# Starting the operands of the 512-column products at multiples of 512 bytes in each SBUF partition

## The chip, the cores and the metric

The kernel runs on one core of a Trainium2 chip. The metric is the time of one execution on the device in microseconds (us); lower is better. SBUF is the on-chip memory: 128 partitions, each a row of bytes, in which every tile of this program has a start address that is the same in all partitions. TensorE (PE in the profile) reads both operands of a product from there.

## The reference

One decoder layer over 2,048 tokens of width 1,024 and 16 meta tokens put ahead of them, all in float32:

```python
h = layer_norm(jnp.concatenate([meta, x], axis=1), ln_in_g, ln_in_b)
mix = hybrid_mixer(h, ...)      # sliding-window attention || gated linear attention, then w_out
h = layer_norm(ALPHA * h + mix, ln1_g, ln1_b)
ffn = swiglu(h, w_gate, w_up, w_down)       # silu(h @ w_gate) * (h @ w_up) @ w_down, width 2816
h = layer_norm(ALPHA * h + ffn, ln2_g, ln2_b)
return h[:, N_META:]
```

The mixer projects every token to 2,320 columns (queries, keys and values of both kinds of attention, an output gate and a low-rank decay gate), runs window attention with eight query heads over a window of 128 tokens and gated linear attention with four heads in chunks, and projects the 1,024 joined columns with w_out.

## The kernel before, in words

**Products in three parts.** Each float32 operand is split into a high part (fp32r) and the rest (`split_into`, L177 to L179: ScalarE writes the high part, VectorE or GpSimd the difference). A product is then three matmuls per 128 rows of the contraction: high by high, high by low, low by high (`matmuls`, L183 to L186, is the one place that issues them, so nearly all carry the line L186 in the profile). A matmul names the stationary operand, 128 columns or 512 bytes of a partition, which a weight load (PEld) brings into the array, and then the moving operand, in most cases 512 columns or 2,048 bytes, that streams through it.

**Stages.** Window attention comes first (to about 430 us): for each block of 512 tokens the products `pu` of the projections, whose moving operand is `h` and whose stationary one is `hl_u`. Linear attention with the output projection follows (to about 1,000 us; `pv`, `po` with 256 or 272 columns, and `pu` again, now on `gh`). The gate and up products of the feed-forward layer run from there to 1,861 us, for two halves of the tokens and 11 pairs of column tiles each; they use seven quarter products (Strassen's method in Winograd's form) with the factors b11, t2, t1, b21, t3, t4, b22 of the tokens as moving operands, in this order, and the weights' factors `pa..`, `ps..` as stationary ones. One quarter product is two chains of 12 matmuls. The last stage is the down projection (1,874 to 2,359 us), with the products `d`: moving operand `B` (weights), stationary operand `A` (activations), and for the pair left over `E`, which holds both.

**Where tiles lie.** The program takes its tiles from pools, and these are stacked in SBUF: most from the left, that is from the end of a scratch area for DMA descriptors at address 0 upwards, some from the right (`side="right"`), from byte 229,344 downwards. A tile takes a multiple of 32 bytes. On the left come, in this order:

- the scratch area, 16,384 bytes, and four constants of the framework with 32 bytes each;
- `cp`: `ident` 512, `neghalf`, `half` and `warm` 32 each, `hm` 1,024, `kTm` 128, in all 1,760 bytes;
- `wpool` (L190) with the staging tiles `x` and the split weights `whl` (tiles `hl_..`, `pa..`, `ps..`, `B`), and `hb` (L209) with two tiles of 16,384 bytes, in turn the tokens `h` and `gh` and the factors b11 and t2. All of these are multiples of 512 bytes, so they begin at 16,384 + 128 + 1,760 = 18,272 = 35 x 512 + 352 and keep the remainder 352;
- after them the pools of the stage: `gp` (4,416 bytes with constants), then `hp1` (L254) with the tokens of every second block; later `fp` and `hop1` (factors t1, b21), and in the last stage `rp` (21,120 bytes) and `dp` with `rA`, `A` and `E`.

On the right lie `gm` (the mixed heads `msh`, `msl`) and, in the gate and up stage, `hop2` (t3, t4) and `hop3` (b22). 229,344 is 447 x 512 + 480.

So each operand of the 512-column products has a remainder on division by 512 (all of them leave 32 on division by 64):

| operand | pool | remainder before |
|---|---|---|
| stationary weights `hl_u`, `pa`, `ps`; moving `B` | wpool | 352 |
| moving `h` of blocks 0 and 2, `gh`, b11, t2 | hb | 352 |
| moving `h` of blocks 1 and 3 | hp1 | 160 |
| moving t1, b21 | hop1 | 352 |
| moving t3, t4, b22 | hop2, hop3 | 480 |
| stationary `A`; both operands in `E` | dp | 480 |

**In the names of the profile**, `t<-h_t,ps` are the products of t2, t1 (remainder 352) and t3 (480), `b<-h_b,pa` those of b11 and b21 (352), `t<-h_t,pa` those of t4 (480) and `b<-h_b,ps` those of b22 (480).

**The order of the work.** The steps of the attention stages are strings written by hand (L36 to L47), and the order on each engine comes from a planner that simulates the program (`schedule_with_timeline_sim=True`). With `reuse_waits="tile"` a tile of a new pool waits for the tiles of an older pool whose bytes it covers.

Of the kernel before, what the change touches and what calls it, by code (L numbers as in the profile page):

```python
# [14 lines left out]
P = 128  # L15
# [12 lines left out]
LEVELS = [64, 32, 16, 8, 4, 2]  # L28
UNITS = ["k_s", "v_s", "q_s0", "q_s1", "q_s2", "q_s3", "q_g0", "q_g1", "k_g0", "k_g1", "r0", "r1", "r2", "r3"]

# The order of the steps for one block of tokens, each with its number.
# Window attention: q projection of a head pair (q this block's, Q the next one's), K keys (0) and
# values (1) of the next block, S scores and V values of a group of heads, L load of a token tile,
# G projection for the linear attention.
WINDOW_STEPS = "G0 L0 S0 V0 q3 S1 L1 L2 q2 S2 V1 G3 S3 G2 G1 V2 L3 K0 V3 Q0 Q1 K1"
# Linear attention: k a chunk's next part; of the next block H load, a and b values, g gate, c its sums,  # L36
# r output gate, m meta tokens; of this block S and G the mixed heads; of the block before
# x output projection, y norm, z transposition; C factors and F first steps of the feed-forward layer.
# [6 lines left out]
# The first products of the feed-forward layer, and what is left of the last block after each.  # L45
# [36 lines left out]
def host_layout(inp):  # L82
# [15 lines left out]
    # the low rank part of the gate, then the values  # L98
# [12 lines left out]
    # quarters (f half, k half) of each pair of f tiles, gate and up side by side  # L111
    gu = np.stack([f(n)[0].reshape(2, KT // 2, P, NP, 2, P) for n in ("w_ffn_gate", "w_ffn_up")])
    a["w_gu"] = gu.transpose(4, 5, 1, 3, 0, 2, 6).reshape(NP, 2, 2, P, D)
    # quarters (f half, output half) of each pair of f tiles
# [7 lines left out]
def body(ctx, tc, t, seq):  # L122
# [34 lines left out]
    def moments(sm, xt, n, name):  # L157
        """-mean * rstd, rstd"""
        st = sm(f"st_{name}", [P, 2, 6])
        for c in range(2):  # L160
            nc.vector.bn_stats(st[:n, c, :], xt[:n, c * 512 : (c + 1) * 512])
        mv = sm(f"mv_{name}", [P, 2])
        nc.vector.bn_aggr(mv[:n], st[:n].rearrange("p a b -> p (a b)"))
        v = sm(f"lv_{name}", [P, 1])
        nc.vector.tensor_scalar(v[:n], mv[:n, 1:2], EPS_LN, None, op0=ALU.add)
        r = sm(f"lr_{name}", [P, 1])
        nc.gpsimd.tensor_tensor(r[:n], v[:n], neghalf[:n, 0:1], op=ALU.pow)
        m = sm(f"lm_{name}", [P, 1])
        nc.vector.tensor_scalar(m[:n], mv[:n, 0:1], r[:n, 0:1], -1.0, op0=ALU.mult, op1=ALU.mult)
        return m, r  # L170

    def normalise(sm, xt, n, name, mr=None):
        """(x - mean) * rstd in place"""
        m, r = mr or moments(sm, xt, n, name)
        nc.scalar.activation(xt[:n], xt[:n], AF.Identity, bias=m[:n, 0:1], scale=r[:n, 0:1])

    def split_into(hi, lo, src, lo_eng=None):  # L177
        nc.scalar.activation(hi, src, AF.Copy)  # L178
        (lo_eng or nc.vector).tensor_tensor(lo, src, r32(hi), op=ALU.subtract)  # L179

# [8 lines left out]
    kTm = cp.tile([P, 2, NM], F32, name="kTm")  # L189
    wpool = ctx.enter_context(tc.tile_pool(name="wpool", bufs=1))  # L190
# [17 lines left out]
    # two halves of 16 KB a partition: a block's tokens by k's halves, then factors, then results  # L208
# [5 lines left out]
    def at(h, a, k):  # L214
        """part a of the tokens' rows k.."""
        return h[k // 4][:, a, k % 4]
# [35 lines left out]
    # ------------------------------------------- input norm and sliding window  # L252
    with ExitStack() as c1:
        hps = [hb, c1.enter_context(tc.tile_pool(name="hp1", bufs=1))]  # L254
        mp = c1.enter_context(tc.tile_pool(name="mp", bufs=1))
# [46 lines left out]
        # a head's values have zeros beside them, in the place of the other head's  # L302
        vhl = [mp.tile([P, NB, 3, 64], F32R, name=f"v{x}") for x in "hl"]
        # the keys of a block and the block before share their slots: what a slot holds
        # of the block before is weighed with the difference of the two blocks' values
# [80 lines left out]
        def begin(u, h):  # L386
            """the first half of a projection, before the other half's tokens are there"""
# [28 lines left out]
        def k_write(raw, n, w, c0, c1_):  # L416
            """both halves of the keys' parts, from [128 (head, d), n * w]"""
# [65 lines left out]
        def swa_scores(s, k, qs):  # L483
            """four heads of two token tiles; a head pair's keys and values lie side by side"""
# [114 lines left out]
    # --------------------------------------------- gated linear attention, output projection  # L599
    # The feed-forward products are taken by quarters, in the seven  # L600
    # multiplications of Strassen's method in Winograd's form.  The tokens'
    # factors: b11, b21, b22 are quarters (k half, token half), t2 = b22 - b12 + b11,
    # t1 = b12 - b11, t3 = b22 - b12, t4 = b21 - t2.
# [7 lines left out]
    def quarter(tb, kh, th, k, n):  # L611
        """rows k.. of one quarter of the tokens, transposed"""
# [4 lines left out]
    def combine(tb, k, tile_):  # L617
        """the sums and differences among the factors, for one of the rows"""
# [20 lines left out]
    def make(f, tb):  # L639
        """a factor of the tokens' side, in its two parts"""  # L640
# [72 lines left out]
    class Mixed:  # L713
        """the mixed heads, in two parts each, and their projection, step by step"""
# [75 lines left out]
    class Project:  # L790
        """the projections of the linear attention for one block of tokens, step by step"""
# [42 lines left out]
        def values(self, blk, n):  # L834
            """the values of one token tile, or of the meta tokens"""
# [39 lines left out]
        def m(self, _):  # L875
            """the state after the meta tokens"""
# [144 lines left out]
    def start_ffn(n):  # L1021
        """the first factors of the feed-forward layer, and the first product"""
# [11 lines left out]
    def take(what, *who):  # L1034
        """one step, of the first that has it; nothing where there is no such block"""
        for x in who:
            if hasattr(x, what[0]):
                return getattr(x, what[0])(int(what[1]))
# [30 lines left out]
    # ------------------------------------------------------------- ffn, gate and up  # L1069
    banks = [0]  # L1070

    def bank(name):
        """the next of the eight banks in turn"""
# [5 lines left out]
    # products of the down projection, in the order taken  # L1079
# [18 lines left out]
    def a_factors(tb, p0, npr):  # L1098
        """the factors of the activations, by tokens' and f's halves"""
# [4 lines left out]
    def combined(b11, b12, b22, b21, t1):  # L1104
        """the factors of the weights, by f's and outputs' halves, one after the other"""
# [20 lines left out]
    def odd_factors(tb):  # L1126
        """the factors of the pair left over, of the activations and of the weights side by side"""
# [15 lines left out]
    def residual(tb, n, i, j, tag):  # L1143
        """alpha times the first norm's output less its bias, one half of a token tile"""
# [7 lines left out]
    def finish(tb, n, i, y, sums, eng):  # L1152
        """norm of one token tile, g2 having the root of D in it"""
# [82 lines left out]
    # quarters of the result that a product ends  # L1236
# [17 lines left out]
    def start_down():  # L1254
        """what the down projection needs before its first product"""
        for n in ("rp", "dp"):
            pools[n] = hops2.enter_context(tc.tile_pool(name=n, bufs=1, reuse_waits="tile"))
        for x, src in (("g1", "ln1_g"), ("b1", "ln1_b"), ("g2", "ln2_g"), ("b2", "ln2_b")):
            rows_[x] = pools["rp"].tile([P, D], F32, name=x)
        for k in range(LOOK):  # L1260
# [42 lines left out]
    # the last block's steps after the first products  # L1303
# [8 lines left out]
    def finish_mixing(f):  # L1312
# [8 lines left out]
        ops.update({f: make(f, 0) for f in ("t3", "t4", "b22")})  # L1321

# [65 lines left out]
    # ------------------------------------------------------------------ ffn, down  # L1388
    pools["acc"] = hops2.enter_context(tc.tile_pool(name="accp", bufs=1, side="right", reuse_waits="tile"))
    ready_to = LOOK  # L1390
    for k, (tb, gi, q) in enumerate(STEPS):
        # of the activations' factors four fit, those left over counted
# [31 lines left out]
```

## Time and profile before

| what | value |
|---|---|
| median of 3 runs | 2394.92 us (2389.49 to 2397.25) |
| span of the profiled execution, first to last instruction | 2381.3 us |
| difference of the two, which lies around the span | 13.6 us |
| PE busy | 2212.6 us, 93%, 11,536 matmuls |
| VectorE busy | 1782.8 us, 75% |
| GpSimd busy | 1613.5 us, 68% |
| ScalarE busy | 957.8 us, 40% |
| mean granted TensorE clock | 0.972 |

The profiled execution has no device time of its own beside its span, so the median stands in for it. Matmuls overlap: the next one starts before the last one's results are out, and the end in the profile contains the way through the array. The pace of a run of matmuls is therefore read from starts: from the start of one group to the start of the next, divided by the number of matmuls between.

### The profile page before, as it was taken

The numbers are of one execution on the slowest core, as the hardware profiler recorded it, in microseconds if no ns is written. First come the engines' busy times: TensorE is split into PE (matmuls) and PEld (weight loads), VectorE is DVE, ScalarE is ACT, GpSimd is POOL, SyncE is SP. The second block draws the span as 40 slices with busy tenths as digits, with TensorE's granted clock in tenths as the row PEclk, the third lists the DMA queues.
The fourth block names the chain that finished last, engine by engine and source line by source line (L and its number), as shares of the span: only waits on it lengthen the run. The fifth ranks groups of instructions, "written<-read, shape, count | busy, mean of one in ns | idle before, by whom it ended". The sixth has DMA issues, their size and how long they took to land.

```text
span 2381.3 us, 32174 instructions
## 1 busy us (share of the span) xinstructions
PE 2212.6 (93%) x11536; PEld 1875.2 (79%) x11536; DVE 1782.8 (75%) x2653; ACT 957.8 (40%) x1606; POOL 1613.5 (68%) x1128
## 2 busy tenths in 40 slices
PE   6999999999999988998999999999999799878995
PEld 5888888888989877976888887888888688656774
DVE  6787765678778696467666667666666689999998
ACT  5565655544353535332222334222323433244332
POOL 6889865848366564565767777767667645895567
PEclk9999999999999999998999999999999899999998
DMA  8754631624363556455323344323223755445532
GB/s 272 231 173 143 213 128 50 214 76 169 126 242 112 213 175 246 167 186 183 124 75 125 106 139 140 129 75 124 97 103 106 267 157 162 135 147 178 175 98 84
DMA packets 169889, 361.01 MB, mean 152 GB/s; under 512 B 15697, under 2 KB 61682, under 8 KB 169730
## 3 DMA queue, kind: packets, MB, share of 16 engines
q1 hardware_dynamic: 165922, 356.51, 44.2%
q10 hardware_dynamic: 3808, 2.45, 0.3%
q8 instruction: 92, 1.51, 0.3%
q14 instruction: 67, 0.55, 0.1%
HBM read 247.22 MB, written 111.67 MB: 151 GB/s over the span
## 4 chain that ended last, share of the span: by engine, by line
PE 58%; DVE 22%; POOL 6%; issue 6%; DMA 5%; ACT 2%; SPq 0%; DVEq 0%; POOLq 0%; ACTq 0%
PE t L186 16%; PE b L186 11%; PE pu L186 8%; PE d L186 6%; PE po L186 6%; PE pv L186 3%; DVE y L1141 3%; DVE xq L963 2%; DVE B L179 2%; DVE A L179 1%; PE oa L550 1%; DMA cb<-n_scT 1%; DVE c L1141 1%; PE lp L969 1%; DVE cb L626 1%
## 5 line engine op out<-in xcount | busy, mean ns | idle before, releaser
L186 PE MATMUL d<-B,A 128*128 128x512 f32 x1680 | 411.8, 401 | 35.9 <-ACT A L178 12.7
L186 PEld LDWEIGHTS d<-B,A 128*128 128x128 f32 x1680 | 321.4, 192 | 116.8 <-ACT A L178 13.2
L186 PE MATMUL t<-h_t,ps 128*128 128x512 f32 x1584 | 375.2, 394 | 11.5 <-DVE ps L179 5.9
L186 PEld LDWEIGHTS t<-h_t,ps 128*128 128x128 f32 x1584 | 298.0, 189 | 79.0 <-DVE ps L179 6.4
L186 PE MATMUL pu<-h,hl_u 128*128 128x512 f32 (+1 forms) x1008 | 247.4, 390 | 2.3 <-ACT hl_u L178 0.9
L179 POOL TENSOR_TENSOR pa<-a,pa 128x1024 fp32r<-128x1024 f32 x65 | 169.1, 2602 | 118.5 <-ACT pa L178 118.4
L186 PE MATMUL b<-h_b,pa 128*128 128x512 f32 x1032 | 241.8, 390 | 0.0
L186 PEld LDWEIGHTS b<-h_b,pa 128*128 128x128 f32 x1032 | 193.6, 188 | 40.7
L186 PE MATMUL po<-hl_o,msh 128*128 128x256 f32 x1024 | 203.6, 295 | 6.1 <-POOL hl_o L179 3.6
L186 PEld LDWEIGHTS pu<-h,hl_u 128*128 128x128 f32 x1008 | 179.8, 193 | 33.7 <-ACT h L178 1.1
L186 PEld LDWEIGHTS po<-hl_o,msh 128*128 128x128 f32 x1024 | 166.4, 196 | 7.5 <-POOL hl_o L179 4.4
L178 ACT ACTIVATE ps<-a 128x1024 fp32r<-128x1024 f32 x66 | 69.9, 1059 | 253.5 <-POOL a L1282 186.7
L178 ACT ACTIVATE A<-rA 128x1024 fp32r<-128x1024 f32 x70 | 74.0, 1059 | 196.0 <-PE d L186 166.4
L186 PE MATMUL po<-hl_o,msl 128*128 128x256 f32 x512 | 149.7, 292 | 0.0
L179 POOL TENSOR_TENSOR hl_u<-st_u,hl_u 128x1024 fp32r<-128x1024 f32 x48 | 116.9, 2438 | 36.5 <-ACT hl_u L178 36.0
L186 PE MATMUL t<-h_t,pa 128*128 128x512 f32 x528 | 128.8, 399 | 4.0 <-POOL pa L179 2.3
L1349 DVE TENSOR_TENSOR u<-u,t 128x512 f32<-128x512 f32 x132 | 89.4, 679 | 52.1 <-PE t L186 52.1
L186 PE MATMUL b<-h_b,ps 128*128 128x512 f32 x528 | 127.1, 395 | 0.0
L186 PEld LDWEIGHTS t<-h_t,pa 128*128 128x128 f32 x528 | 100.1, 190 | 28.9 <-POOL pa L179 2.8
L963 DVE TENSOR_TENSOR xq<-e,gqk 64x128 f32<-64x128 f32 x224 | 119.6, 534 | 3.1 <-PE lp L969 0.2
L186 PEld LDWEIGHTS b<-h_b,ps 128*128 128x128 f32 x528 | 99.1, 188 | 24.0
L1299 DVE SCALAR_TENSOR_TENSOR sb<-sb,u 128x512 f32<-128x512 f32 x22 | 50.4, 2290 | 89.7 <-ACT sb L1298 89.6
(337 smaller groups left out, 5294.0 us busy)
## 6 DMA issues: line engine op xcount, KB each, us to landing
a<-w_gu SPq DMA_DIRECT2D x88, 512.0 KB, 4.3
rA<-a_sc SPq DMA_DIRECT2D x70, 512.0 KB, 3.9
st_u<-w_u SPq DMA_DIRECT2D x56, 512.0 KB, 4.2
x<-w_d SPq DMA_DIRECT2D x40, 512.0 KB, 3.7
hT_sc<-h SPq DMA_DIRECT2D x32, 512.0 KB, 4.5
gh<-hT_sc SPq DMA_DIRECT2D x16, 1024.0 KB, 9.3
st_o<-w_o SPq DMA_DIRECT2D x32, 512.0 KB, 4.7
a_sc<-sa SPq DMA_DIRECT2D x44, 256.0 KB, 4.2
```

What stands on the lines that cost most here:

```text
L178: nc.scalar.activation(hi, src, AF.Copy)
L179: (lo_eng or nc.vector).tensor_tensor(lo, src, r32(hi), op=ALU.subtract)
L186: nc.tensor.matmul(out, l, r, start=(i == 0), stop=(i == n - 1))
L550: nc.tensor.matmul(oa[:, n], l, m, start=False, stop=(hh == 1 and i == 5))
L626: nc.vector.tensor_tensor(o, x, y, op=how)
L963: nc.vector.tensor_tensor(x[rows[hh], :, hh, :].rearrange("p j (b c) -> p j b c", c=c), eq[rows[hh]], qv[rows[hh], :, :, 1, :], op=ALU.mult)
L969: nc.tensor.matmul(o[:, P * j : P * j + P], kl[:, j, :], x[:, j].rearrange("p h q -> p (h q)"), start=True, stop=True)
L1141: (eng or nc.vector).tensor_tensor(o, x, y, op=ALU.add)
L1299: nc.vector.scalar_tensor_tensor(tt, tt, 1.0, g, op0=ALU.add, op1=ALU.mult)
L1349: nc.vector.tensor_tensor(o[i], x[i], y[i], op=ALU.add)
```

## The change

Four tiles that nothing reads or writes are allocated, so that the tiles behind them begin elsewhere: 160 bytes at the end of `cp`, 192 ahead of the tiles of `hp1`, 480 in `hop2` (on the right, so that `hop2` and with it `hop3` lie lower) and 384 ahead of the tiles of `dp`. The scratch area for DMA descriptors has 8,192 bytes in place of 16,384. All comments are taken out, which changes no instruction.

```diff
+PADS = {"cp": 160, "hp1": 192, "right": 480, "dp": 384}
...
+    def pad(pool, n, name):
+
+        return pool.tile([P, n // 4], F32, name=name)
...
     kTm = cp.tile([P, 2, NM], F32, name="kTm")
+    pad(cp, PADS["cp"], "pad_cp")
     wpool = ctx.enter_context(tc.tile_pool(name="wpool", bufs=1))
...
         hps = [hb, c1.enter_context(tc.tile_pool(name="hp1", bufs=1))]
+        pad(hps[1], PADS["hp1"], "pad_hp1")
...
             rows_[x] = pools["rp"].tile([P, D], F32, name=x)
+        pad(pools["dp"], PADS["dp"], "pad_dp")
...
         ops.update({f: make(f, 0) for f in ("t3", "t4", "b22")})
+        pad(pools["hop2"], PADS["right"], "pad_hop2")
...
-    nc = bacc.Bacc("TRN2", target_bir_lowering=False, num_devices=1)
+    nc = bacc.Bacc("TRN2", target_bir_lowering=False, num_devices=1, dynamic_dma_scratch_size=8192)
```

The remainders of the table become 0 throughout: 18,272 - 8,192 + 160 = 10,240 = 20 x 512 for `wpool` and `hb`; 4,416 + 192 = 9 x 512 ahead of `h` in `hp1`; 229,344 - 480 - 32,768 = 383 x 512 for `hop2`; and 21,120 + 384 = 42 x 512 ahead of the tiles of `dp`. The left side as a whole lies 8,032 bytes lower, the right side stays apart from the 480 bytes. `gm` gets no such bytes: `msh` and `msl`, the stationary operands of `po`, keep the remainder 480.

## The prediction

> **What bounds the kernel now.** I read the page's busy times first, then the chain of work that ended last, then a table of stretches, and last the timeline of single runs of matmuls, because the change can act only on the pace of matmuls.
>
> ```profile
> PE 2212.6 (93%) x11536; PEld 1875.2 (79%) x11536; DVE 1782.8 (75%) x2653; ACT 957.8 (40%) x1606; POOL 1613.5 (68%) x1128
> ...
> PE 58%; DVE 22%; POOL 6%; issue 6%; DMA 5%; ACT 2%; SPq 0%; DVEq 0%; POOLq 0%; ACTq 0%
> PE t L186 16%; PE b L186 11%; PE pu L186 8%; PE d L186 6%; PE po L186 6%; PE pv L186 3%; DVE y L1141 3%; DVE xq L963 2%; DVE B L179 2%; DVE A L179 1%; PE oa L550 1%; DMA cb<-n_scT 1%; DVE c L1141 1%; PE lp L969 1%; DVE cb L626 1%
> ```
>
> PE is the busiest engine and holds 58% of the chain, but that is an average over stages. Four stretches show their different limits: the columns are the length, then PE, PEld, DVE, ACT and POOL busy with the count of instructions, then the granted clock, the DMA share and GB/s.
>
> ```profile
> 200.00:400.00 200.00, 192.09 (x1150) 168.52 (x1150) 132.16 (x351) 111.77 (x286) 147.20 (x106) 1.00 0.42 134
> 1260.00:1360.00 100.00, 100.00 (x437) 81.59 (x436) 70.17 (x68) 27.68 (x35) 67.89 (x32) 1.00 0.28 98
> 1880.00:1960.00 80.00, 80.00 (x346) 64.87 (x345) 63.28 (x68) 35.86 (x44) 41.37 (x18) 1.00 0.56 183
> 2000.00:2200.00 200.00, 170.44 (x692) 133.96 (x691) 195.19 (x206) 79.26 (x101) 145.55 (x70) 0.94 0.50 159
> ```
>
> In the gate and up stage (second row) PE never rests, at full clock, and no other engine exceeds 70.17 of 100 us: there each nanosecond per matmul counts in full. In window attention (first row) PE has small holes. In most of the down projection (last row) DVE is busy for 195.19 of 200 us and PE rests; only its first 80 us (third row) are PE's.
>
> **The pace, by where operands begin.** The timeline gives the start and length of each run of matmuls, here in the gate and up stage:
>
> ```profile
> 1227.32 5.76 PE L186 MATMUL t<-h_t,pa 128*128 128x512 f32 x24
> 1232.92 5.76 PE L186 MATMUL b<-h_b,ps 128*128 128x512 f32 x24
> 1238.52 5.62 PE L186 MATMUL b<-h_b,pa 128*128 128x512 f32 x24
> 1243.97 1.30 PE L186 MATMUL t<-h_t,ps 128*128 128x512 f32 x5
> ```
>
> From start to start, t4 and b22 take 5.60 us for 24 matmuls, 233.3 ns each; b11 takes 5.45, 227.1 ns each. Shape, engine and clock are the same. What differs is where the moving operand begins: remainder 480 for t4 and b22, 352 for b11, and the stationary one has 352 in both. So the place matters, by 6.2 ns. Other stages, read in the same way:
>
> ```profile
> 328.24 0.28 PE L550 MATMUL oa<-pch,vl 128*128 128x256 f32 x1
> 328.36 0.28 PE L550 MATMUL oa<-pcl,vh 128*128 128x256 f32 x1
> 328.48 5.89 PE L186 MATMUL pu<-h,hl_u 128*128 128x512 f32 x25
> 334.21 0.28 PE L550 MATMUL oa<-pbh,vdh 128*128 128x256 f32 x1
> ...
> 2249.73 39.36 PE L186 MATMUL d<-B,A 128*128 128x512 f32 x168
> 2288.93 0.86 PE L186 MATMUL d<-E 128*128 128x512 f32 x3
> 2289.63 0.62 PE L186 MATMUL d<-B,A 128*128 128x512 f32 x2
> ...
> 2312.00 1.48 PE L186 MATMUL d<-E 128*128 128x512 f32 x3
> 2313.28 2.10 PE L186 MATMUL d<-B,A 128*128 128x512 f32 x6
> ...
> 2311.20:2313.70 2.50, 2.50 (x7) 1.94 (x6) 2.50 (x3) 0.00 (x0) 2.50 (x2) 0.50 0.00 0
> ```
>
> `pu` on block 3 (160 against 352) takes 5.73 / 25 = 229.2 ns; `d` (352 against 480) 39.20 / 168 = 233.3; `E` (480 against 480) 0.70 / 3 = 233. At half the granted clock (last row, 0.50) three `E` take 1.28 us, 426.7 ns each; half of that is 213.3 ns, the pace that the array alone would set at full clock. So 14 to 20 ns of each 512-column matmul are not the array's, and that is all there is to win. By how much a start at 512 shortens them no row shows, since no such operand begins there. The nearest rows are transpositions against products of 128 columns:
>
> ```profile
> L442 PE MATMUL vt<-ident,vraw 128*128 128x128 f32 x16 | 2.6, 272 | 0.0
> L545 PE MATMUL oa<-ptm,vbd 128*128 128x128 f32 x128 | 19.7, 275 | 0.3 <-DVE kTm L412 0.3
> ```
>
> `ident` is the moving operand of the first and lies at 16,512, a multiple of 128; `ptm` leaves 96. The first takes 272 ns, the second 275: 3 ns for one operand's start, though the two also differ in kind. After the change both operands of a 512-column product begin on a boundary. I therefore take 2 x 3 = 6 ns off the better of today's paces: 227.1 - 6 = 221.1 ns for all of them. The ends are 213.3 (nothing is left over the array's time) and 227.1 (only equal remainders count, as in b11). Below, I also price a loss.
>
> **The sum.** The counts and busy times:
>
> ```profile
> L186 PE MATMUL d<-B,A 128*128 128x512 f32 x1680 | 411.8, 401 | 35.9 <-ACT A L178 12.7 <-DVE y L1141 11.0 <-DVE A L179 4.7
> L186 PE MATMUL t<-h_t,ps 128*128 128x512 f32 x1584 | 375.2, 394 | 11.5 <-DVE ps L179 5.9 <-DVE c L1349 3.8 <-POOL ps L179 1.2
> L186 PE MATMUL pu<-h,hl_u 128*128 128x512 f32 (+1 forms) x1008 | 247.4, 390 | 2.3 <-ACT hl_u L178 0.9 <-ACT h L178 0.7 <-DVE h L179 0.7
> L186 PE MATMUL b<-h_b,pa 128*128 128x512 f32 x1032 | 241.8, 390 | 0.0
> L186 PE MATMUL po<-hl_o,msh 128*128 128x256 f32 x1024 | 203.6, 295 | 6.1 <-POOL hl_o L179 3.6 <-DVE yo L757 2.0 <-ACT p L1353 0.4
> L186 PE MATMUL po<-hl_o,msl 128*128 128x256 f32 x512 | 149.7, 292 | 0.0
> L186 PE MATMUL t<-h_t,pa 128*128 128x512 f32 x528 | 128.8, 399 | 4.0 <-POOL pa L179 2.3 <-POOL h_t L179 1.7
> L186 PE MATMUL b<-h_b,ps 128*128 128x512 f32 x528 | 127.1, 395 | 0.0
> L186 PE MATMUL pu<-gh,hl_u 128*128 128x512 f32 x384 | 94.6, 398 | 0.2 <-POOL hl_u L179 0.2
> ```
>
> *Gate and up.* A third of the 1584, 528, is t3; with t4 and b22 that makes 1584 matmuls at 233.3 ns: 1584 x 12.2 = 19.3 us. The other 1056 and b11 and b21's 1032 run at 227.1: 2088 x 6.0 = 12.5 us. Together 31.8 us, all on the path, since PE is full and DVE, next, has 30 us free in 100.
>
> *The products `pu`.* Blocks 1 and 3 have ten units of 24 matmuls each, 480 at 229.2: 480 x 8.1 = 3.9 us; the other 912 give 912 x 6.0 = 5.5. The chain holds 8% of 2381.3 = 190 us of `pu`, of 247.4 + 94.6 = 342 us busy, 56%: 5.3 us count.
>
> *Down.* 1848 x 12.2 = 22.5 us of PE time, but DVE ends last there. I count only the stretch that is PE's: 346 x 12.2 = 4.2 us. The bounds are 0 and the chain's 6%, 143 of some 465 us: 31% of 22.5, 7.0 us.
>
> *Narrow products.* `po` has 256 columns; at 328.24 and 328.36 such matmuls start 120 ns apart, with 106.7 as the array's share. Its moving operand moves to 0, but its stationary one keeps 480: 3 ns x 1536 = 4.6 us, of which the chain's 6% (143 of 353 us busy) lets 40% through: 1.8 us, with 0 and twice that as bounds, or a loss of as much, since its two remainders, 128 apart before, are 32 apart then.
>
> Sum: 31.8 + 5.3 + 4.2 + 1.8 = 43 us. Median and span differ by 13.6 us, which stays: 2394.9 - 43 = 2352 us.
>
> *The rest of the edit.* The padding tiles add no instruction, and no step moves by hand. Two rows show why the scratch area is worth nothing either way:
>
> ```profile
> q1 hardware_dynamic: 165922, 356.51, 44.2%
> q10 hardware_dynamic: 3808, 2.45, 0.3%
> ```
>
> Besides instruction fetches these are all the queues there are, and no DMA is issued on GpSimd. But the left side lies 8,032 bytes lower against the right, so some tiles cover other old tiles, and waits with them. The largest place is the first product of the down projection:
>
> ```profile
> PE d L186 <- ACT A L178: 12.7, 1, 12.7
> ...
> 1867.18 5.75 DMA rA<-a_sc
> ```
>
> PE waits 12.7 us there for `A`, whose load was issued at 1867.18, behind others in SP's queue; all of `d` stands behind it. It is a matter of order more than of memory, so I price it at nothing; it could give or take up to 12.7 us, and I keep 5 either way for the range, the planner's order included.
>
> [...] The trace's paces differ by 6.2 ns at starts that are all multiples of 32 bytes. [...]
>
> **The rivals.**
>
> *No change (17%).* The pace hangs on something that goes with the pool and not with the remainder: t3, t4 and b22 also lie highest in SBUF. Then nothing moves but waits: 2395 us, 2388 to 2402. [...] For it: `E` has equal remainders and is no faster than `d`. Against it: `pu` at 160 and `d` at 352 against 480 lie elsewhere and also miss 227.1.
>
> *Only equal remainders count (22%).* All run at b11's 227.1: 1584 x 6.2 = 9.8 us in gate and up, 480 x 2.1 x 56% = 0.6 for `pu`, 346 x 6.2 = 2.1 for `d`: 12.5 us, 2382 us. For it: the best row has them equal. Against it: `E` again.
>
> *Everything at the array's pace (inside the forecast's chance).* 1584 x 20.0 + 2088 x 13.8 = 60.5; `pu` (480 x 15.9 + 912 x 13.8) x 56% = 11.3; `d` 346 x 20.0 = 6.9; `po` 1536 x 6.6 x 40% = 4.1: 83 us, 2312 us. [...]
>
> *Slower (13%).* Both operands of every product begin at the same place of a 512-byte stretch, and weights are loaded while the previous matmul streams; if the two reads then meet more often, all run like the worst of today, 233.3: 2088 x 6.2 = 12.9 in gate and up, (480 x 4.1 + 912 x 6.2) x 56% = 4.3 for `pu`, nothing for `d`: 17 us more, 2412 us. For it: `E`, equal remainders and 233. Against it: b11, equal and best. It decides from a common pace over (1584 x 233.3 + 2088 x 227.1) / 3672 = 229.8 ns.
>
> **How the numbers follow.** Forecast, a common pace clearly under 227.1, 48%, its own range 2312 to 2372; equal remainders only 22%; no change 17%; slower 13%. The three runs before spread over 0.3%, so 0.3%, 7 us, is about what can be told from no change. The first two cases are faster by more: 70%. The range must leave out no more than 2 in 10: from the array's end, 2312 less some 5 us for waits, to 2404, which takes in no change with its waits and leaves out most of the slower case.
>
> **What would show it.** In the timeline after, runs of 24 in the gate and up stage: at 221 ns the start distance is 5.31 us for every factor; 5.45 for all means equal remainders only; 5.60 for t4 and b22 alone, no effect; 5.60 for all, the loss. PE should hold more matmuls in 100 us, 452 for 437, with DVE near 72. In the down projection DVE's busy time should stay and PE's idle time grow. The forecast is wrong if the pace is over 225, or if the pace falls and the gate and up stage does not shorten by its sum.

## The result and the profile after

The changed kernel takes 2401.5 us, median of five runs (2399.84 to 2405.24); the kernel before 2394.92 in the same session. The ratio is 1.0034, 95% interval 1.0018 to 1.0051: slower, by an amount that a measurement of this kernel can just tell from nothing. The forecast was 2352 us. Beside the four groups of experiments below the kernel before had medians of 2389.1 to 2392.5 us; the changed kernel was not run again with them, so each ratio below is to the kernel before of its own group. The page of the profile after begins so (the span, the busy times, then the chain that ended last):

```profile
span 2403.4 us, 32183 instructions
...
PE 2205.0 (92%) x11536; PEld 1878.5 (78%) x11536; DVE 1773.1 (74%) x2653; ACT 954.6 (40%) x1606; POOL 1613.0 (67%) x1128
...
PE 43%; DVE 24%; POOL 13%; issue 9%; DMA 7%; ACT 3%; SPq 0%; DVEq 0%; POOLq 0%; ACTq 0%
```

Two things are to be seen. PE is busy 7.6 us less than before (2205.0 against 2212.6), so its matmuls did get faster, and yet the span grew. And on the chain PE fell from 58% to 43%, while POOL rose from 6% to 13%: for long stretches the chain that ended last no longer runs along PE, which is almost as busy as before, but through the work that feeds it. The profiled execution's own time is 2405.24, so some 1.9 us lie around its span. That of before spans 2381.3 us, which with 1.9 us around it would be below all five of its runs beside the changed kernel's; the 22 us between the two spans overstate the 7 between the medians.

**The pace.** In the timeline after, all factors of gate and up run alike; the columns are start, length, engine, line, operation and count:

```profile
1067.37 5.60 PE L192 MATMUL b<-h_b,pa 128*128 128x512 f32 x24
1072.81 5.60 PE L192 MATMUL t<-h_t,ps 128*128 128x512 f32 x24
1078.24 5.60 PE L192 MATMUL t<-h_t,pa 128*128 128x512 f32 x24
```

From start to start 5.44 us for 24, 226.7 ns each: what b11 had before, and no more. Even a full window holds 443 matmuls, 6 more than before and not the 452 of the forecast (columns as in the prediction's stretches):

```profile
1260.00:1360.00 100.00, 100.00 (x443) 82.81 (x442) 69.91 (x71) 28.26 (x36) 70.39 (x32) 1.00 0.33 116
```

**Where the time went.** Starts of first products, taken from the traces, cut the span into seven stretches. The third column is a second profile of the very program of before (experiment e6), which shows how far two executions differ anyway. The last cut but one is the start of the last factor's second chain of 12 matmuls, called the last factor from here on:

| stretch, us | before | before, again | after |
|---|---|---|---|
| start to the last block's first `po` | 943.3 | 947.0 | 951.3 |
| to the first product of pair 4 of gate and up | 218.1 | 219.1 | 225.5 |
| six plain pairs, 4 to 10 | 231.4 | 231.4 | 228.5 |
| boundary of the token halves, three pairs | 121.2 | 123.4 | 130.1 |
| plain pairs of the second half, to the last factor | 344.3 | 344.3 | 340.0 |
| last factor to the first product of down | 15.8 | 16.8 | 20.5 |
| down projection to the end | 507.2 | 506.8 | 507.5 |

The plain pairs give what equal paces make: 0.5 us a pair. Everything around them takes it back, and more: the start of gate and up (+7.4), the boundary of the halves (+8.9) and the start of the down projection (+4.7); against the second profile of before they are +6.4, +6.7 and +3.7. The first row's differences can't be put down to the change: two profiles of one program (e1 and e5) got there in 949.0 and 946.0, and a kernel with other remainders than before (e7) in 943.1.

At the start of gate and up the first product of t3 ran from 1009.52 before:

```profile
1009.52 3.65 PE L186 MATMUL t<-h_t,ps 128*128 128x512 f32 x15
```

After the change it stands at 1031.23:

```profile
1020.15 0.66 PE L778 MATMUL nt<-ident,yo 128*128 128x128 f32 x4 [0.20 <-ACT ntr L780]
1024.25 2.84 PE L778 MATMUL nt<-ident,yo 128*128 128x128 f32 x12 [3.44 <-ACT ntr L780]
1031.23 6.77 PE L192 MATMUL t<-h_t,ps 128*128 128x512 f32 x20 [4.14 <-ACT h_t L180]
```

PE first ends all transpositions (`nt`), waits between them for ScalarE's copies, and only then gets t3's factor. The order of the instructions shows why. Before, t3's tile takes exactly the bytes 196,576 to 212,960 that `msl` had. With 480 bytes ahead of it, it begins at 196,096 and reaches into `ntr` (190,432 to 196,576), which is in use until the last z step. So the planner puts the making of t3, t4 and b22 behind that step; elsewhere the order of the matmuls is that of before.

At the boundary of the halves PE waits for split weights. Before, the two longest waits there are 1.17 and 2.33 us:

```profile
1438.59 10.72 PE L186 MATMUL t<-h_t,ps 128*128 128x512 f32 x46 [1.17 <-POOL ps L179]
1463.15 6.93 PE L186 MATMUL t<-h_t,pa 128*128 128x512 f32 x22 [2.33 <-POOL pa L179]
```

After, it waits more often and for longer:

```profile
1445.61 5.28 PE L192 MATMUL b<-h_b,pa 128*128 128x512 f32 x22 [1.65 <-POOL pa L181]
1457.62 1.22 PE L192 MATMUL t<-h_t,ps 128*128 128x512 f32 x2 [6.74 <-ACT ps L180]
1460.79 12.67 PE L192 MATMUL t<-h_t,ps 128*128 128x512 f32 x46 [1.95 <-POOL ps L181]
```

And at the start of the down projection it waits 17.68 us where it waited 12.7:

```profile
1895.91 2.07 PE L192 MATMUL d<-B,A 128*128 128x512 f32 x4 [17.68 <-ACT A L180]
```

### The profile page after: what moved, and what is told of

It is laid out like the page before. It is cut to its first block, busy times and chain, and to the rows that moved or that the text cites. A ratio compares the mean times of both kernels' runs of the same rounds, so it can differ in the third digit from the quotient of the medians.

```text
span 2403.4 us, 32183 instructions
## 1 busy us (share of the span) xinstructions
PE 2205.0 (92%) x11536; PEld 1878.5 (78%) x11536; DVE 1773.1 (74%) x2653; ACT 954.6 (40%) x1606; POOL 1613.0 (67%) x1128
## 4 chain that ended last, share of the span: by engine, by line
PE 43%; DVE 24%; POOL 13%; issue 9%; DMA 7%; ACT 3%; SPq 0%; DVEq 0%; POOLq 0%; ACTq 0%
PE t L192 9%; PE pu L192 7%; PE b L192 6%; PE d L192 6%; PE po L192 5%; PE pv L192 3%; DVE y L1149 3%; DVE xq L971 2%; POOL a L1291 2%; DVE B L181 2%; POOL pa L181 2%; DMA cb<-n_scT 1%; DVE A L181 1%; DVE c L1149 1%; PE oa L558 1%
## 5 line engine op out<-in xcount | busy, mean ns | idle before, releaser
L181 POOL TENSOR_TENSOR pa<-a,pa 128x1024 fp32r<-128x1024 f32 x65 | 161.9, 2491 | 127.5 <-ACT pa L180 127.5
L181 POOL TENSOR_TENSOR hl_u<-st_u,hl_u 128x1024 fp32r<-128x1024 f32 x48 | 117.6, 2453 | 38.6 <-ACT hl_u L180 37.5
L1291 POOL TENSOR_TENSOR a<-a,a 128x1024 f32<-128x1024 f32 x44 | 114.1, 2594 | 1.7
```

The source lines that it names most:

```text
L1291: sub = lambda o, x, y: nc.gpsimd.tensor_tensor(o, x, y, op=ALU.subtract)
```

## The experiments

Two theories stood first. *Cover*: the 480 bytes in `hop2` change the order and cost more than the pace gives. *Pace*: a shorter PE only meets the other engines' work sooner, so that equal remainders gain nothing or lose. Later runs test a third, *preparation*: the steps that make the split weights have a pace of their own, just under that of the matmuls.

**e1, the right side moved from the top instead.** A pool opened ahead of `gm` takes the 480 bytes at the top of the right side. All remainders 0 (those of `po`'s operands too), the order on every engine that of before:

```diff
-        pad(pools["hop2"], PADS["right"], "pad_hop2")
+    rt = ctx.enter_context(tc.tile_pool(name="rt", bufs=1, side="right"))
+    rt.tile([P, 120], F32, name="pad_rt")
```

> The 480 bytes are taken at the very top of the right side, ahead of gm, go, hop2 and hop3 alike, so that every operand has remainder 0 (po's stationary one too) and t3 covers exactly the bytes of msl again, as in the kernel before. Theory 'cover' (the 480 bytes made t3 reach into one of z's buffers ntr, and the wait for it cost more than the pace gave): the order of the products is that of before, the pace 226.7 ns for all, and the time about 12 us under the kernel before, 2380 to 2387 us. Rival 'pace' (a shorter PE only meets other engines' work sooner, so that equal remainders gain nothing or lose): 2395 us or more, as after the change.

Measured: 2390.99 us, ratio 1.0002 (0.9989 to 1.0015). The loss is gone, so it lay in the place of those 480 bytes. But no gain appears, though the products of gate, up and down run at 226.7 to 227.2 ns, and the time misses the 2380 to 2387 us of *cover*: that is half of the answer, and that the pace gains nothing is still to be explained.

**e2, the 480 bytes alone.** The kernel before with the small scratch and these bytes only:

```diff
         ops.update({f: make(f, 0) for f in ("t3", "t4", "b22")})
+        pools["hop2"].tile([P, 120], F32, name="pad_hop2")
```

> The kernel before with a scratch area of 8,192 bytes and the 480 bytes in hop2, and no other padding. Theory 'cover': the late start of t3, t4 and b22 comes back in full, with none of the paces in d and pu gained: slower than the kernel before by 10 to 20 us, 2405 to 2415 us. Rival 'pace': no slower than before, 2389 to 2397 us, since no product has gained equal remainders.

Measured: 2402.38 us, ratio 1.0056 (1.0044 to 1.0067), a little less than the 2405 to 2415 expected. The order on every engine is that of the changed kernel, and the timeline has the same late t3:

```profile
1023.78 3.15 PE L770 MATMUL nt<-ident,yo 128*128 128x128 f32 x12 [3.64 <-ACT ntr L772]
1030.78 8.21 PE L186 MATMUL t<-h_t,ps 128*128 128x512 f32 x20 [3.85 <-ACT h_t L178]
```

Cover is shown: these bytes alone make a loss as large as the whole one. The small scratch has no part in it, since e3 has it too and loses nothing. t3, t4 and b22 run at 234.1 to 234.3 ns here, with moving operands at 0 against weights at 352.

**e3, the change without the 480 bytes.** Left side at 0, t3, t4 and b22 still at 480:

```diff
-        pad(pools["hop2"], PADS["right"], "pad_hop2")
```

> The changed kernel without the 480 bytes: t3, t4 and b22 keep remainder 480 against weights at 0, all others have 0. Theory 'cover': no late start; d and pu at 226.7 ns, t3, t4 and b22 near 233; 2 to 4 us under the kernel before, 2390 to 2394 us. Rival 'pace': as slow as after the change, 2398 to 2405 us, since the shorter d and pu are still there.

Measured: 2387.12 us, ratio 0.9989 (0.9976 to 1.0002), not to be told from the kernel before and a little under the range of *cover*. t3, t4 and b22 stay at 233.3 to 233.4 ns against weights at 0, `d` falls from 232.6 to 227.0.

**e4, all remainders 352.** As e1, with no bytes in `cp` and 128 on top of the right side:

```diff
-    pad(cp, PADS["cp"], "pad_cp")
-    rt.tile([P, 120], F32, name="pad_rt")
+    rt.tile([P, 32], F32, name="pad_rt")
```

> All operands of the 512-column products with remainder 352 instead of 0 (no bytes in cp, 128 at the top of the right side, the rest as in the first kernel). If only equal remainders count: the same pace, 226.7 ns, and the same time as the first kernel within 3 us. If the start at a multiple of 512 bytes is worth something of its own: slower than the first kernel by 5 us or more, with a pace above it.

Measured: 2388.08 us, ratio 0.9994 (0.9986 to 1.0003), and 226.7 to 227.2 ns in gate, up and down: the multiple of 512 itself is worth nothing.

**e5 and e6, an edit that did nothing.** I had read the timeline of e1 as a ring: GpSimd waits some 3.75 us a pair for a load that is issued when GpSimd has let go of a staging tile:

```profile
1667.44 2.39 POOL L1297 TENSOR_TENSOR s<-a,a 128x1024 f32<-128x1024 f32 x1 [3.75 <-DMA a<-w_gu]
```

The edit was to let a22 and a12 change places in odd pairs, in the kernel of e1 and in that of before:

```diff
-        for a, (i, j) in (("a11", (0, 0)), ("a21", (1, 0)), ("a22", (1, 1)), ("a12", (0, 1))):
+        for a in ("a11", "a21") + (("a12", "a22") if p % 2 else ("a22", "a12")):
             raw[a] = fp.tile([P, D], F32, tag="x2", name=f"{a}_{nm}", bufs=4)
+        for a, (i, j) in (("a11", (0, 0)), ("a21", (1, 0)), ("a22", (1, 1)), ("a12", (0, 1))):
             nc.sync.dma_start(raw[a], t["w_gu"][p, i, j])
```

> The kernel with the bytes on top of the right side (all remainders 0, order as before), and in every odd pair of gate/up the staging tiles of a22 and a12 change places, so that a22's load waits for the old a12 (last read by VectorE about 1658.9 us in the run with the bytes on top) and not for the old a22 (read by GpSimd until 1663.7). Order on all engines as in the run without it. Theory 'ring': the preparation of the weights is a ring through ScalarE, VectorE, GpSimd and SP's queue with a period of its own of 37.8 us a pair; matmuls at 38.1 a pair build up almost no lead over 10 pairs (GpSimd's sum of a21 and a22 stands 47.4 us ahead of its pair's first product at pair 4 and 47.6 at the end of the half; before 47.4 and 57.9), and the lead is what pays for the two boundaries. With the ring some 2 us shorter (about 36) the lead grows to 57 or more by the end of the first half, the boundary costs about 5 us over the plain pairs in place of 14.7, the down projection starts 10 to 16 us after the last group in place of 20.7: 2370 to 2380 us, ratio to before 0.991 to 0.995. Rival 'matmuls bound the stage, the boundaries lose time by where the tiles lie': 2387 to 2394, boundaries as they were.

> The kernel before with only the change of places of a22 and a12 in odd pairs (scratch and remainders as before, order on all engines as before). Theory 'ring': the lead at the end of the first half grows from 57.9 us to 60 or more where the split tiles' four buffers cap it, and from 53 to about 58 at the end of the second half; the boundary between the halves costs 1 to 4 us over plain pairs in place of 5.5, the down projection starts about 11 us after the last group in place of 15.7: 2385 to 2391 us, ratio 0.996 to 0.999. Rival 'matmuls bound the stage': 2393 to 2397, ratio 1.000.

Measured: 2388.72 (1.0000, 0.9989 to 1.0011) and 2391.71 us (1.0007, 0.9994 to 1.0020). The framework did not give out the tiles in the order of the calls: it gave each quarter the place it had, and both programs are, instruction by instruction and address by address, those of e1 and of before. They test nothing of the ring and serve as repeats. One slip of the expectation is to be mended too: the 47.4 and 47.6 us run from GpSimd's sum of one pair to the first product of the *next* pair. In this sense the word lead is used below.

**e7, all remainders 480.** 128 bytes in `cp` and the right side not moved at all:

```diff
-PADS = {"cp": 160, "hp1": 192, "right": 480, "dp": 384}
+PADS = {"cp": 128, "hp1": 192, "right": 480, "dp": 384}
-        pad(pools["hop2"], PADS["right"], "pad_hop2")
```

> Scratch 8192, left side padded by 128 in place of 160 bytes, hp1 192 and dp 384, right side not moved at all: every operand of the 512-column products has remainder 480, order on all engines as before. Theory 'equal remainders': all gate/up and down products at 226.7 to 227.0 ns as at 0/0 and 352/352. Rival 'the place counts, not the equality': the products of E stood at 480/480 before with 231.9 ns, so all of gate/up and down run at 231 to 234, 39.2 us a pair, and the kernel takes 2397 to 2405 us. Theory 'ring' with equal remainders fast: about 2388, as the runs with all at 0 or 352; 'moved right side costs 6 to 9 us at the boundary between the halves': 2380 to 2384.

Measured: 2390.31 us, ratio 0.9998 (0.9985 to 1.0012):

```profile
1252.56 5.60 PE L192 MATMUL b<-h_b,pa 128*128 128x512 f32 x24
1258.00 5.60 PE L192 MATMUL t<-h_t,ps 128*128 128x512 f32 x24
1263.44 5.60 PE L192 MATMUL t<-h_t,pa 128*128 128x512 f32 x24
1268.88 5.60 PE L192 MATMUL b<-h_b,ps 128*128 128x512 f32 x24
```

5.44 us for 24 again, so 480 is as good as 0 and 352, if both operands have it. `E`, at 480/480 as before, has 227.7 ns here and had 232.2: before, its runs of three stood between `d` at 352/480 (here all are equal), and what the neighbours' remainders do to it is the likeliest reason. e8 fits: there `E` has 320/320 between `d` at 0/320, and 232.1 ns. The boundary costs 16.4 us over plain pairs, though nothing on the right moved: its cost does not come from tiles moved there.

**e8, one distance per factor.** All at 0 but the moving operands of t1 (32), t3 (64), t4 (128), b22 (256), b21 (384), and `A` and `E` at 320. As e1, with

```diff
+    AHEAD = {"t1": 32, "b21": 352, "t3": 64, "t4": 64}
...
+            if tb == 0 and f in AHEAD:
+                pad(pool, AHEAD[f], f"pad_{f}")
...
+        pad(pools["hop2"], 384, "pad_hop2")
+        pad(pools["hop3"], 256, "pad_hop3")
```

and 320 bytes more in `dp`, 512 more in `gm`.

> All remainders 0 but for the moving operands of some factors: t1 at 32, t3 at 64, t4 at 128, b22 at 256, b21 at 384, A at 320 with B at 0, E with both at 320. One profile, read for the pace of each group alone. Theory 'equal remainders': 226.7 ns for b11, t2 and E, 230 to 234 for all the others. Rival 'the place of each operand counts': some places between are as fast as 0 though the other operand lies at 0, and E at 320/320 may be slow. Rival 'distance modulo 64': only t1 is slow.

Measured: 2396.90 us, one run, for its pace only. The rows are b11, t2 with t1, b21, t3, t4, b22, and the next b11:

```profile
1243.46 5.60 PE L192 MATMUL b<-h_b,pa 128*128 128x512 f32 x24
1248.90 11.21 PE L192 MATMUL t<-h_t,ps 128*128 128x512 f32 x48
1259.94 5.74 PE L192 MATMUL b<-h_b,pa 128*128 128x512 f32 x24
1265.52 5.67 PE L192 MATMUL t<-h_t,ps 128*128 128x512 f32 x24
1271.02 5.75 PE L192 MATMUL t<-h_t,pa 128*128 128x512 f32 x24
1276.61 5.63 PE L192 MATMUL b<-h_b,ps 128*128 128x512 f32 x24
1282.07 3.11 PE L192 MATMUL b<-h_b,pa 128*128 128x512 f32 x13
```

From start to start: b11 5.44, t2 and t1 11.04, b21 5.58, t3 5.50, t4 5.59, b22 5.46. Means over some 500 intervals each: 226.7 to 227.1 ns at distance 0, 233.3 at 32, 229.4 at 64, 232.7 at 128, 227.7 at 256, 232.3 at 384, 233.3 for `d`, whose stationary operand is the one at 320. For these products of 512 columns equal remainders are best, 256 apart is nearly as good, and distance modulo 64 is refuted.

**e9, a longer preparation.** The kernel before, with GpSimd's last step of each pair done twice (the second writes the same values):

```diff
             nc.gpsimd.tensor_tensor(s4, c21, sc[:, 1], op=ALU.subtract)
+            nc.gpsimd.tensor_tensor(s4, c21, sc[:, 1], op=ALU.subtract)
```

> The kernel before with GpSimd's last step of each pair of gate/up (the difference s, 1.3 us) done twice, 22 times in all: 28 us more for an engine that is busy 68 per cent. Theory 'preparation': the steps that make the split weights on GpSimd, ScalarE and SP's queue take 37.8 us a pair of their own, 0.8 less than the matmuls' 38.6, and this surplus is the lead that pays for the boundaries. With 1.25 us more a pair (39.1) the lead falls instead of growing, and the end of each half comes 5 to 12 us later: 2405 to 2418 us, ratio 1.006 to 1.012. Rival 'matmuls bound the stage': GpSimd's idle time takes it in, within 3 us of before, ratio 0.999 to 1.002.

Measured: 2414.31 us, ratio 1.0100 (1.0078 to 1.0121): 22 steps of 1.3 us, 28 us of work on an engine that is busy 68%, cost 22 to 24 us. The sums `s` of one pair each, in before, in after and in e9 (first and last start, with their count):

```profile
L1286 POOL TENSOR_TENSOR s<-a,a x6: 2401/2858/2956, 1504.8 to 1694.4; 128x1024 f32<-128x1024 f32 x6
```

```profile
L1295 POOL TENSOR_TENSOR s<-a,a x6: 2387/2505/2904, 1527.2 to 1716.4; 128x1024 f32<-128x1024 f32 x6
```

```profile
L1286 POOL TENSOR_TENSOR s<-a,a x7: 2395/2581/2950, 1154.7 to 1389.7; 128x1024 f32<-128x1024 f32 x7
```

GpSimd comes round every 189.6 / 5 = 37.9 us before, 37.8 after, and 235.0 / 6 = 39.2 in e9. PE needs 38.6 a pair before and 38.1 after. In e9 the matmuls, which alone would need 38.6, fall into step at 39.2, with a small wait in every pair:

```profile
1285.99 10.74 PE L186 MATMUL t<-h_t,ps 128*128 128x512 f32 x46 [0.30 <-POOL ps L179]
...
1325.34 10.74 PE L186 MATMUL t<-h_t,ps 128*128 128x512 f32 x46 [0.30 <-POOL ps L179]
```

*Matmuls bound the stage* is refuted: the preparation is less than 1 us a pair behind, and what it is faster, it saves up as lead. This lead pays for the boundary, as all runs with four staging tiles show in which the boundary's own work is that of before (cost: three pairs there, less three plain ones of the first half):

| run | lead at the boundary, us | boundary's cost, us |
|---|---|---|
| before | 57.9 | 5.5 |
| e3 | 57.2 | 5.9 |
| e6 | 55.5 | 7.7 |
| e8 | 54.7 | 8.7 |
| e2 | 53.0 | 11.4 |
| e5 | 51.1 | 13.7 |
| e4 | 48.8 | 15.4 |
| after | 48.2 | 15.9 |
| e7 | 48.0 | 16.4 |
| e1 | 47.6 | 14.8 |
| e9 | 47.6 | 20.0 |

Lead and cost add up to 62 to 65 us in every row but the last, whose preparation is longer by itself: a microsecond of lead saves about one of the boundary. Faster matmuls keep the lead small: 0.5 us a pair saved is 0.5 us a pair less lead. At the end of the second half it is 53.0 before and 48.1 after, and the first product of down comes 15.8 and 20.5 us after the last factor.

**e10 and e11, GpSimd spared at the boundary.** In the second half's factors VectorE takes all low parts; e10 with all remainders 480, e11 in the kernel before:

```diff
-            split_into(x[:, 0, k], x[:, 1, k], raw, nc.vector if k % 2 else nc.gpsimd)
+            split_into(x[:, 0, k], x[:, 1, k], raw, nc.vector if k % 2 or tb else nc.gpsimd)
```

> All remainders 480 (as in the run with equal remainders at 480), and in the second half's factors VectorE takes all the low parts, GpSimd none (14 steps of 1.3 to 1.75 us, some 21 us, go from GpSimd at the boundary between the halves to VectorE at about 0.7 each). Order of the matmuls as before. Theory 'preparation': the boundary costs 14 us over plain pairs with equal remainders because GpSimd's steps for the new factors delay the split weights (its pairs take 41 and 52 us there in place of 37.8); with 21 us fewer the cost falls by 8 to 14 us, and the kernel takes 2376 to 2383 us, ratio 0.994 to 0.997. Rival 'the boundary waits for the factors' loads or for something else': the boundary as it was, 2387 to 2393.

> The kernel before (scratch, bytes and remainders as before) with the same shift of the second half's low parts to VectorE. Theory 'preparation': the boundary costs 5.5 to 7.6 us over plain pairs before, 0 to 3 here: 2384 to 2389 us, ratio 0.997 to 0.9985; and the kernel with equal remainders and the same shift is 4 to 8 us faster than this one, the matmuls' 0.5 us a pair, which the boundary no longer takes back in the first half. Rival: as the kernel before, 2388 to 2393, and no difference between the two.

Measured: 2388.19 us, 0.9983 (0.9970 to 0.9997), and 2388.43 us, 0.9989 (0.9975 to 1.0003). A miss: 21 us less work of GpSimd shorten its two pairs at the boundary only from 41.1 + 52.6 us (e7) to 41.3 + 50.5, and the boundary by 3 us in e10 (13.6) and by nothing in e11 (7.0, at a lead of 55.9). Nor do the two differ: the pace's gain stays lost. So GpSimd's own steps are not the main thing that holds the preparation up there. In e1 ScalarE stood idle in front of a load of the new factors:

```profile
1417.76 0.63 ACT L180 ACTIVATE h_b<-r_b 128x512 fp32r<-128x512 f32 x1 [9.41 <-DMA r_b<-n_scT]
```

Whether such loads set the boundary's cost was not tried.

**e12, six staging tiles.** All remainders 480 as in e7, and the 8,192 bytes that the smaller scratch leaves go to the weights' staging:

```diff
-        x = pool.tile([P, D], F32, tag=tag, name=f"{tag}_{p0}", bufs=4)[:, : npr * W]
+        x = pool.tile([P, D], F32, tag=tag, name=f"{tag}_{p0}", bufs=6 if tag == "x2" else 4)[:, : npr * W]
...
-            raw[a] = fp.tile([P, D], F32, tag="x2", name=f"{a}_{nm}", bufs=4)
+            raw[a] = fp.tile([P, D], F32, tag="x2", name=f"{a}_{nm}", bufs=6)
```

> All remainders 480, and six staging tiles for the weights in place of four (8,192 bytes, those that the smaller scratch leaves free). The planner's order changes: 131 of SP's 897 steps and 96 of the matmuls stand elsewhere, most by one or a few places. Theory 'preparation': GpSimd waits 3.4 to 3.9 us a pair for a load that is issued only when a staging tile is free; with two more the load is there, the preparation takes about 34 us a pair until the four split tiles stop it, the lead is 57 or more at the end of each half: boundary 4 to 8 us in place of 14, start of the down projection 4 us earlier, 2374 to 2383 us, ratio 0.993 to 0.997. Rival 'another link sets the 37.8 us' (ScalarE behind VectorE behind ScalarE): GpSimd's pairs stay at 37.8, 2387 to 2393.

Measured: 2376.83 us, ratio 0.9939 (0.9922 to 0.9957). GpSimd's wait for the load ahead of `s` sums to 0.4 us in a window of seven pairs, where it was 26.4 after:

```profile
L1295 POOL TENSOR_TENSOR s<-a,a x7: 2389/2402/3402, 1149.8 to 1368.7; 128x1024 f32<-128x1024 f32 x7
...
  DMA a<-w_gu: 0.4, 1
```

Over these pairs the sums come every 218.9 / 6 = 36.5 us, and where the lead still grows, from pair 3 to 5 of the second half, every 34.3 and 34.4. The lead is 63.4 us at both ends, the boundary costs 8.7 and down starts 14.1 us after the last factor. The boundary does not fall to nothing: with leads of 63 to 65 it costs 7.0 to 9.0 in e12 to e15, a part that the lead does not pay. The kernel beats both others.

**e13, e14, e15, what is worth what then.** The same kernel again (e13); six tiles with the small scratch and the remainders of before (e14), the order on every engine that of e13; six tiles with the change as it was made (e15). To e14's and e15's kernels e12's edit is made, in e14 to the kernel before with

```diff
-    nc = bacc.Bacc("TRN2", target_bir_lowering=False, num_devices=1)
+    nc = bacc.Bacc("TRN2", target_bir_lowering=False, num_devices=1, dynamic_dma_scratch_size=8192)
```

> The kernel with six staging tiles and all remainders 480 once more, as the common measure of the next two. Expected 2373 to 2380 us, ratio 0.992 to 0.996, as in its first run.

> Six staging tiles, scratch 8192, no bytes left free: remainders as in the kernel before (352, 160, 480), order on all engines that of the run with six tiles and equal remainders. Theory 'preparation': with the lead of 57 us or more the matmuls set the pace of gate/up, so the remainders now count: 38.6 in place of 38.1 us a pair over 17 plain pairs (8 us), and 0.9 us in each of the 7 groups of the down projection that VectorE does not bound: 6 to 14 us slower than with equal remainders, 2382 to 2390 us, ratio 0.996 to 0.999. Rival 'the gain of the six tiles is all there is': as with equal remainders, 2374 to 2379.

> The change as it was made (all remainders 0 but po's, 480 bytes in hop2, so that t3's tile reaches into ntr), with six staging tiles. Theory 'cover': t3's factor is made after the last z step, and the first pairs lose 5 to 10 us, which no lead can pay: 2381 to 2388 us, ratio 0.995 to 0.998. Rival 'the lead pays for it': with more staged weights the later start is made up by the boundary, 2374 to 2380 us, as with all remainders 480.

Measured: e13 2376.87 us, 0.9947 (0.9934 to 0.9960); e14 2385.83, 0.9981 (0.9970 to 0.9991); e15 2385.68, 0.9985 (0.9974 to 0.9995). The chain of e13 has PE back at 58%:

```profile
PE 58%; DVE 22%; DMA 7%; POOL 5%; issue 5%; ACT 3%; SPq 0%; DVEq 0%; POOLq 0%; ACTq 0%
```

e14 and e13 differ in the remainders alone, and equal ones are worth 9 us between the medians. Their profiles put it where the sum had it: from pair 4 to the last factor 690.8 us against 698.4, and from there to the end 517.2 against 518.4. The lead is 63 to 65 us in both. And the 480 bytes in `hop2` cost 8.8 us between the medians here too (e15 against e13), at a lead of 63.4 us: no lead pays for them.

## Why the prediction was wrong

**The pace: 221.1 ns forecast, 226.7 measured.** The step that failed is "2 x 3 = 6 ns off the better of today's paces". The two rows that it rested on, 272 and 275 ns, were of products of another kind, and they were durations, not paces: back to back, the starts of these matmuls lie 109 and 111 ns apart. The rival *only equal remainders count* named the right pace, and I held `E` against it. `E` misled: three matmuls at a time between unequal neighbours are no measure of a pace. Two times 3 ns also took the two starts as free of each other, and the traces do not bear that out: 226.7 ns at equal remainders stand against 232.7 at 128 bytes apart (b11 and t4 in e8). Where the time goes stays open.

**"... all on the path, since PE is full and DVE, next, has 30 us free in 100."** This is the step that cost the gain. With the right pace the rival had 9.8 us for gate and up, and the plain pairs gave 7.2 of them (2.9 + 4.3). But no engine has to be full for a chain through several engines to be the bound: GpSimd is busy 68 of 100 us there and comes round every 37.8 us all the same, since it waits in every pair for ScalarE and for a load that waits for it (in the seven pairs from 1149 us of after, 42.4 us ahead of `pa` and 26.4 us ahead of `s`). PE at 38.6 was the slower of the two by less than 1 us. The gain of the pairs was taken back where the lead is spent: 8.9 us at the boundary, 4.7 at the start of down (6.7 and 3.7 against the second profile of before). e9 shows the limit, e14 against e13 the gain when it is lifted.

**"It is a matter of order more than of memory, so I price it at nothing."** This is the step that made a loss of it: it was a matter of memory first. I looked for the danger on the left side and at the first product of down; it lay in `hop2`, where t3's tile fitted the bytes of an old tile exactly and 480 bytes pushed it into one that is freed later. That costs 9.3 us in one pair at the start of gate and up (42.1 us where it took 32.8), and 12 us between the medians of e2 and the kernel before.

**Down, `pu` and `po`.** The down projection's PE-bound groups fell from 39.0 to 38.1 us, near the 2.1 us in 80 of the rival. Over the stage nothing is left of it in the two profiles (507.2 and 507.5), but these are not typical: the other nine profiles with equal remainders in `d` (e1, e3, e4, e5, e7, e10, e12, e13, e15) have 503.9 to 506.1 us there, the six others with unequal ones 506.3 to 508.5, about the 2 us that the rival had. Of `pu` no gain can be told from what two executions differ by. The pace of `po`, which has 256 columns, did fall, from a mean of 119.2 ns to 116.9, near the 3 ns of the forecast, but by luck. In the timeline after, 15 of them take 1.75 us:

```profile
1004.76 0.39 PE L192 MATMUL po<-hl_o,msh 128*128 128x256 f32 x2
...
1006.51 0.40 PE L192 MATMUL po<-hl_o,msh 128*128 128x256 f32 x2
```

In e1, where both operands of `po` begin at 0, nine take 1.08 us, 120 ns each:

```profile
1004.74 0.40 PE L192 MATMUL po<-hl_o,msh 128*128 128x256 f32 x2
...
1005.82 0.28 PE L192 MATMUL po<-hl_o,msh 128*128 128x256 f32 x1
```

So it was not the start at a multiple of 512 that made `po` faster. Its means are 116.9 to 117.2 ns with remainders 32 apart (after, e3, e15) and 119.6 to 119.7 with equal ones (e1, e4, e5, e7, e8, e10, e12, e13): here equal remainders are the slower ones. Why these products differ from those of 512 columns was not tried.

**The scratch area** was rightly priced at nothing by itself (e3 and e7 have the small one and take what the kernel before takes); its bytes, put to use, brought the best version.

**What the sum stood on.** The 13.6 us between median and span do not lie around the span: where the record has both times of an execution, 1.7 to 3.6 us do, and the rest was a profiled execution faster than the median. That 2401.5 us lies inside the stated range, whose top is 2404, is luck: the top was set for no change with its waits, and a better pace together with a dearer order is none of the cases.

## What to carry to other kernels

Try the same remainder modulo 512 for both operands of a stream of 512-column matmuls (226.7 ns here against up to 234.3; which one did not matter), and read the pace of the others by themselves, since `po` with 256 columns was slower with it (119.7 ns against 116.9 at 32 bytes apart); then look at what the bytes moved, since a tile that fits exactly over an old one can lose its place in the order when it reaches into the next, here by 480 bytes. And before a gain on a full engine is counted, read the period of the chain that feeds it: the time from the first to the last start of one recurring step, divided by the number of rounds between, tells it, and a busy share does not.

## What the runs showed of the hardware

A 512-column matmul of gate, up and down takes 226.7 to 227.2 ns where its two operands, and those of its neighbours, have equal remainders (0, 352 and 480 alike in e1, e4 and e7; `E`, in runs of three, up to 227.7), 227.7 with 256 bytes between them, 229.4 with 64 (both e8), and 232.3 to 234.3 with 32, 128, 320, 352 or 384 (before, e2, e3, e8). The 256-column matmuls of `po` go the other way: 119.6 to 119.7 ns at equal remainders, 119.2 to 119.4 with 128 bytes between, 116.9 to 117.2 with 32. That the two starts act together is seen in these paces alone; what makes them do so no run shows. The 213.3 ns that the prediction took for the array's own pace is an estimate, half of the 426.7 that three `E` took at half the granted clock in the trace of before; no group read here came nearer to it than 226.7.
